# Loads, vector order and token slots around the last product of a cross-attention output projection

## The chip, the core and the metric

The kernel runs on one core of a Trainium2 chip. The metric is the device time of one execution in microseconds (us), over several runs of the same program. One further execution was taken with the hardware profiler, and every row below comes from it. The engines are called by the profile's names: PE (TensorE), DVE (VectorE), ACT (ScalarE), POOL (GpSimd) and SP (SyncE, which here only issues DMAs).

## What is computed

One encoder layer over 512 tokens of width 1024 in float32. The part that matters here is its last third: memory cross-attention, its output projection `w_xo`, a norm, and a SwiGLU feed-forward network.

```python
def memory_cross_attention(hn, memn, w_q, w_k, w_v, w_o):
    ...
    s = jnp.einsum('blhd,bmhd->bhlm', q, k).astype(jnp.float32) * (XATTN_HEAD_DIM ** -0.5)
    p = jax.nn.softmax(s, axis=-1).astype(v.dtype)
    o = jnp.einsum('bhlm,bmhd->blhd', p, v).reshape(bsz, seq, D_MODEL)
    return o @ w_o

def swiglu(hn, w_gate, w_up, w_down):
    return (jax.nn.silu(hn @ w_gate) * (hn @ w_up)) @ w_down
...
        h = h + memory_cross_attention(rms_norm(h, xattn_norm_g[i]), memn, ...)
        h = h + swiglu(rms_norm(h, ffn_norm_g[i]), w_gate[i], w_up[i], w_down[i])
    return rms_norm(h, final_norm_g)
```

## The kernel before

Every matrix product is made of three matmuls (`mm3`): each operand is split into a high half (`hi`, a cast on ACT, line 85) and a low half (`lo`, a subtraction on DVE, line 86), and hi x hi, hi x lo and lo x hi are summed in PSUM. So each block of weights (512 KB) takes a DMA, a cast of about 1 us and a subtraction of about 1.2 us before PE can use it.

**The plan.** All weight blocks stand in one list, `plan`, in the order in which they are used. `next_w` takes the next block. On its way it starts the loads of later blocks (`begin`: a block of the plan is loaded `LOADS` = 3 positions ahead, those of a feed-forward unit at distances of their own) and splits blocks up to `SPLITS` = 2 positions ahead. `FAR` is how far down the list it looks for loads that are due. Raw blocks share three buffers (tag `raw`), and so do the high and the low halves (tags `hi`, `lo`). The framework's scheduler then orders the instructions of each engine, DMA issues on SP included, by a simulated timeline; `in_order` pins an instruction behind the one written before it on its engine, and `pinned[0]` turns that on for `split` and `sum_sq`.

**The products.** `w_xo` and the feed-forward units are multiplied by a Strassen-like scheme of seven products, P1 to P7, over sums of quarter blocks. `w_xo` takes each product in two halves c, which makes fourteen plan positions, counted here from 0: P1 c0, P7 c0, P1 c1, P7 c1, P6 c0 (4), P5 c0 (5), P6 c1 (6), P5 c1 (7), P4 c0, c1 (8, 9), P2 c0, c1 (10, 11), P3 c0, c1 (12, 13). Behind them stand a block of `w_gate` (14), P1 of feed-forward unit 0 (15), a second block of `w_gate` (16), P2 of unit 0 (17), two blocks of `w_up` (18, 19), and P5 of unit 0 (20). A half product of `w_xo` is 12 matmuls of 512 columns.

The weights of a unit come from four loads: `b11` (P1), `b21` (P2), and `t` and `b22` (P5). `t` is loaded by SP, and a second block is then added onto it by a DMA that POOL issues (line 181). `b21`, `t` and `b22` live in the pool `units`, which is opened where the attention pool `ap_` has been closed and takes its memory. The operands of P5 and P6 of `w_xo` lie in two tiles of `ap_` (`kt_hi`, `kt_lo`), and so `ap_` is closed after P5.

**The norm between.** When both halves of a row of `h` are complete, `half_done` squares them (ACT, line 499). `to_fn` makes the factor (DVE `ms`, POOL `r`), scales the row into `xs` (DVE, line 525), and somewhat later `to_feat` transposes `xs` on PE (`ptr`, line 533, 8 for a token tile) and splits it into `fn_hi` and `fn_lo` (ACT, DVE) and a copy `full` (ACT, line 537). Tokens 0 and 1 (256 rows, T0) come before tokens 2 and 3 (T1). The feed-forward stage begins with half products on T0 alone (`gate_part(0, T0)`, `unit_start`, `gate_part(1, T0)`, `unit_second`, 24 matmuls of 256 columns each), and goes on to T1 after that. `between()` is one matmul whose result is not used.

`fn` and `hn`, like `xn` at the start, are the two views of one tile with the tag "B" (`token_slot`).

**The softmax.** `scores` divides each row of probabilities by its sum on DVE (line 1270), four instructions of 128x256 for a head.

Of the kernel before, what the change touches and what calls it, by code (L numbers as in the profile page):

```python
# [10 lines left out]
F32R = mybir.dt.float32r  # L11
AF = mybir.ActivationFunctionType
# [5 lines left out]
P = 128  # L18
# [34 lines left out]
def hybrid_layer_kernel(  # L53
# [41 lines left out]

    LOADS, SPLITS, FAR = 3, 2, 7
    plan, tiles = [], []

    def block(w, kb, k, c0, n):
# [15 lines left out]
    def halves_at(t, k, n, off):  # L117

        return tuple(t[:, i * k * n + o:(i + 1) * k * n + o].rearrange("p (k n) -> p k n", k=k)
                     for i, o in enumerate(off))  # L120
# [38 lines left out]

    stp = [None]  # L160

    def plan_unit(w, c0, ordered=False):

        kh = KD // 2
        b = lambda i, j: block(w, i * kh, kh, c0 + 256 * j, 256)
        r = {}

        def fresh(nm):
            r[nm] = (wp if nm == "b11" else stp[0]).tile([P, kh, 256], F32, tag="raw" if nm == "b11" else nm,
                                                         name=nm, bufs=3 if nm == "b11" else 2)  # L170
            return r[nm]

        def plain(nm, src):
            def f():
                ins = nc.sync.dma_start(fresh(nm), src)
                if ordered:
                    in_order(ins)
            return f

        def onto(nm, src):  # L180
            return lambda: nc.gpsimd.dma_start(r[nm], src, accum_op=ALU.add)

        def tt(o, x, y, op):
            nc.vector.tensor_tensor(r[o], r[x], r[y], op)

        def make(nm, *then):
            def f():
                ops = halves(r[nm])
                if then:
                    tt(*then)  # L190
                return ops
            return f

        return {q: ((w, c0, q), loads, made) for q, loads, made in (
            (1, [(4, plain("b11", b(0, 0)))], make("b11")),
            (2, [(4, plain("b21", b(1, 0)))], make("b21")),
            (5, [(7, plain("t", b(0, 0))), (5, onto("t", b(0, 1))), (5, plain("b22", b(1, 1)))],
             make("t", "t", "t", "b22", ALU.add)),
            (6, [], lambda: (make("t", "b11", "t", "b11", ALU.subtract)(), tt("t", "t", "b21", ALU.add))[0]),
            (7, [], make("b11")),  # L200
            (4, [], make("t")),
            (3, [], make("b22")))}
# [42 lines left out]
    def plan_units(units, down):  # L245


        made = [plan_unit(*u, ordered=i == 1) for i, u in enumerate(units)]
        for i in range(2):
            plan_block(w_gate, 4 * i, 4, FS, 256, place=i + 1)  # L250
            plan.append(made[0][i + 1])
        plan_feat(w_up, FS, KD)
        for i, m in enumerate(made):
            nx = made[i + 1] if i + 1 < len(made) else {}
            between = [nx[1]] if nx else down[:1]
            plan.extend([m[5], m[6]] + between + [m[7], nx[2] if nx else down[1], m[4], m[3]])
        plan.extend(down[2:])
# [288 lines left out]
    def slot(tag, shape, dt, name):  # L546
        return sp.tile(list(shape), dt, tag=tag, name=name)

    def token_slot(name, off=(0, 0)):

        return halves_at(sp.tile([P, 2 * KD * T + 128], F32R, tag="B", name=name), KD, T, off)


    s5 = ExitStack()
# [589 lines left out]
    h = slot("A", (P, NT, D), F32, "h")  # L1144
    for t in range(NT):
        nc.sync.dma_start(h[:, t, :], x[t * P:(t + 1) * P, :])
    hn_hi, hn_lo = token_slot("hn", APART)

    def mq_tile(name, off):
        return ap_.tile([P, KD * M + 64], F32R, tag="mq", name=name, bufs=2)[:, off:off + KD * M]  # L1150
# [98 lines left out]
    def scores(hd):  # L1249
        q_hi, q_lo = qs.pop(hd)  # L1250
        scale = XD ** -0.5
        prob = ap_.tile([P, NT, M], F32, tag="prob", name="prob", bufs=1) if hd % 2 == 0 else \
            np_.tile([P, NT, M], F32, tag="gain", name="prob", bufs=2)
        for i in range(2):
            ps = bank("psc").rearrange("p (t m) -> p t m", t=2)
            for tt in range(2):
                t = 2 * i + tt
                tsl = slice(t * P, (t + 1) * P)
                for k in range(2):
                    mm3(ps[:, tt, :], (q_hi[:, k, tsl], q_lo[:, k, tsl]),  # L1260
                        (kt_hi[:, 2 * hd + k, :], kt_lo[:, 2 * hd + k, :]), k == 0, k == 1)
            mx, nm, sm, rs = (ap_.tile([P, 2], F32, tag=k, name=k, bufs=4) for k in ("mx", "nm", "sm", "rs"))
            nc.vector.tensor_reduce(mx, ps, AX.X, ALU.max)
            nc.vector.tensor_scalar(nm, mx, -scale, None, ALU.mult)
            for tt in range(2):
                nc.scalar.activation(prob[:, 2 * i + tt, :], ps[:, tt, :], AF.Exp, bias=nm[:, tt:tt + 1],
                                     scale=scale, accum_out=sm[:, tt:tt + 1])
            nc.vector.reciprocal(rs, sm)
            for tt in range(2):
                nc.vector.tensor_scalar(prob[:, 2 * i + tt, :], prob[:, 2 * i + tt, :], rs[:, tt:tt + 1], None, ALU.mult)  # L1270
        return prob

    def turn_probs(hd, prob):
# [138 lines left out]
    def onto(ps, t0, half, op):  # L1412
        for t in range(2):
            hs = h[:, t0 + t, HALF[half]]
            nc.vector.tensor_tensor(hs, hs, ps[t], op)

    def half_done(t, half):
        sum_sq(hss[:, 1, t, half:half + 1], h[:, t, HALF[half]])
# [1 line left out]
    values(0, *pts.pop(0))  # L1420
    probs2 = scores(2)
    probs3 = scores(3)
    for q, nm in ((5, "kt_hi"), (6, "kt_lo")):
        s_ = ap_.tile([P, KD, M], F32R, name=nm).rearrange("p (i k) t -> p i k t", i=2)
        xops[q] = s_[:, 0], s_[:, 1]
    turn(1, probs1)
    ox = [bank("ox0"), bank("ox1")]
    xo_product(ox, 1, 0, True, False)
# [8 lines left out]
    values(3, *pts.pop(3))  # L1437
    xo_product(oy, 7, 1, False, True)
    onto(oy, 0, 1, ALU.subtract)
    oq = [bank("oq0"), bank("oq1")]  # L1440
    xo_product(ox, 6, 0, False, False)
    xo_product(oq, 5, 0, True, False)
    xo_product(ox, 6, 1, False, True)
    onto(ox, 0, 1, ALU.subtract)
    xo_product(oq, 5, 1, False, True)
    at.close()
    ff = ExitStack()
    fp = ff.enter_context(tc.tile_pool(name="ffn", bufs=1))
# [1 line left out]
    sx = ExitStack()  # L1450
    stp[0] = sx.enter_context(tc.tile_pool(name="units", bufs=2))
    full = fp.tile([P, KD, T], F32, tag="full", name="full", bufs=1)
    onto(oq, 0, 1, ALU.add)
    onto(ox, 0, 0, ALU.add)
    for t in range(2):
        half_done(t, 1)
    onto(ox, 2, 1, ALU.subtract)
    xo_product(oy, 4, 0, False, False)
    xo_product(oy, 4, 1, False, True)
    fn_hi, fn_lo = token_slot("fn", APART)  # L1460
    fn = (fn_hi, fn_lo)
    to_fn = feat_norm(g_f, fn_hi, fn_lo, full)
    for t in range(2):
        hs = h[:, t, HALF[0]]
        nc.vector.tensor_tensor(hs, hs, oy[t], ALU.add)
        half_done(t, 0)
        to_fn(t, hss[:, 1, t, :])
    ov = [bank("ov0"), bank("ov1")]
    xo_product(ov, 2, 0, True, False)
    xo_product(ov, 2, 1, False, True)  # L1470
    onto(ov, 2, 0, ALU.add)
    for t in (2, 3):
        half_done(t, 0)

    ws = [next_w(w_xo, 3, c) for c in range(2)]
    for t in range(2):
        for c in range(2):
            xo_product(oq, 3, c, False, c == 1, ws[c], (t,))
        hs = h[:, 2 + t, HALF[1]]
        nc.vector.tensor_tensor(hs, hs, oq[t], ALU.add)  # L1480
        half_done(2 + t, 1)
        to_fn(2 + t, hss[:, 1, 2 + t, :])

# [134 lines left out]
    for i, u in enumerate(UNITS):  # L1620
        final = i == len(UNITS) - 1
        x, v = begun
        q = unit_bank("pq")
        product(q, u, 5, True, ops)
        if final:
            last_job.append(u)
            make_tokens(1, 0)
        if i == 0:
            split(*fn_q(K0, T1), s3)
            between()  # L1630
        product(x, u, 6, False, ops)
        u2 = stp[0].tile([P, 2, 256], F32, tag="u2", name="u2", bufs=2)
        u3 = np_.tile([P, 2, 256], F32, tag="ev", name="u3", bufs=2)
        nc.scalar.copy(u2, x)
        if not final:
            begun = unit_start(UNITS[i + 1])
        else:
            dx = [bank(f"dx{t}") for t in range(2)]
            down_product(dx, 1, True, range(1))
        product(x, u, 7, False, ops)  # L1640
        nc.scalar.copy(u3, x)
        if i == 0:
            sum4()
        if not final:
            unit_second(UNITS[i + 1], begun[1])
        else:
            down_product(dx, 1, True, range(1, 2))
        V.tensor_tensor(u3, q, u3, ALU.subtract)
        put(u, 1, T1, u3)
        product(x, u, 4, False, ops)  # L1650
        put(u, 0, T1, x)
        if u[0] is w_up:
            a_, b_ = (acts(u[1] // 512, f)[:, :, T1] for f in (0, 1))
            V.tensor_tensor(a_, a_, b_, ALU.subtract)
        product(q, u, 3, False, ops)
        V.tensor_tensor(u2, q, u2, ALU.subtract)
        put(u, 1, T0, u2)
# [131 lines left out]
```

## Time and profile before

| | |
|---|---|
| median of 3 runs | 908.13 us (906.52 to 908.89) |
| profiled execution | 908.21 us, of which the span is 906.4 us |
| PE busy | 889.8 us, 98% of the span |
| DVE busy | 643.9 us, 71% |
| ACT busy | 488.1 us, 54% |
| POOL busy | 111.0 us, 12% |
| DMA moved | 165.35 MB, mean 182 GB/s |

Shares are over the whole span. The changed code stands between 505 and 610 us of it: heads 2 and 3 of the softmax at about 515 to 525 us, `w_xo` from 520 to 572 us, and the first feed-forward blocks behind it. A matmul of 512 columns shows 389 to 394 ns from its start to its end, but the next one starts 0.23 us after it, since they are pipelined; rows that join several instructions give the time from the first start to the last end.

### The profile page before, as it was taken

To read this page: it belongs to the slowest core of one execution; us is meant where nothing else is said; L and a number is where in the kernel's file an instruction comes from. 1 tells how busy PE (TensorE), PEld (TensorE's weight loads), DVE (VectorE), ACT (ScalarE), POOL (GpSimd) and SP (SyncE) were. 2 spreads that over 40 slices of the span, in tenths; PEclk is the share of its full clock that TensorE was granted. 3 is DMA by queue.
4 is the path that set the end of the run, shared out by engine and by line. 5 is a ranking of instruction groups with operands and counts; after the bars stand their busy time and mean duration, and the time that the engine had idled before them with its cause. 6 is when DMAs were issued, how large, how long until landed. Compare 5 with 4: busy or idle time off the path is not lost.

```text
span 906.4 us, 14551 instructions
## 1 busy us (share of the span) xinstructions
PE 889.8 (98%) x5620; PEld 785.7 (87%) x5620; DVE 643.9 (71%) x1048; ACT 488.1 (54%) x716; POOL 111.0 (12%) x173
## 2 busy tenths in 40 slices
PE   9999999999999999999999999899999999999996
PEld 6788888888888887889989987799999999988885
DVE  5596662888853125867956898886778777898875
ACT  5542985244375233446655675655554554665664
POOL 1003420110025300011000001101121111000010
PEclk9999999999999999999999999999999999999999
DMA  7556574587546568883569627628698999367672
GB/s 240 164 141 191 119 181 143 156 216 162 140 125 150 135 182 245 247 275 96 163 208 267 175 70 234 208 52 228 166 275 221 212 229 244 96 181 232 201 232 95
DMA packets 116167, 165.35 MB, mean 182 GB/s; under 512 B 13873, under 2 KB 78913, under 8 KB 116034
## 3 DMA queue, kind: packets, MB, share of 16 engines
q1 hardware_dynamic: 95234, 134.56, 45.7%
q0 software_dynamic: 18272, 28.81, 19.4%
q10 hardware_dynamic: 2592, 1.05, 0.5%
q8 instruction: 44, 0.72, 0.3%
q14 instruction: 25, 0.20, 0.1%
HBM read 157.61 MB, written 46.63 MB: 225 GB/s over the span
## 4 chain that ended last, share of the span: by engine, by line
PE 84%; DMA 4%; ACT 4%; DVE 4%; issue 2%; POOL 0%; SPq 0%; ACTq 0%; POOLq 0%; DVEq 0%
PE pf L374 27%; PE px L1301 12%; PE pt L374 11%; PE dx L374 6%; PE pq L1301 6%; PE pv L1301 3%; PE qx L1301 2%; PE dq L374 2%; PE pk L813 2%; PE po L374 1%; PE psc L374 1%; PE qq L1301 1%; PE ptr L533 1%; DVE wlo L86 1%; PE dv L374 1%
## 5 line engine op out<-in xcount | busy, mean ns | idle before, releaser
L86 DVE TENSOR_TENSOR wlo<-wraw,whi 128x1024 fp32r<-128x1024 f32 (+1 forms) x147 | 174.7, 1189 | 106.3 <-ACT whi L85 104.4
L85 ACT CAST whi<-wraw 128x1024 fp32r<-128x1024 f32 (+1 forms) x147 | 150.6, 1025 | 171.7 <-PE pf L374 67.4
L374 PE MATMUL pf<-xn,whi 128*128 128x512 f32 x448 | 140.1, 392 | 0.0
L374 PEld LDWEIGHTS pf<-xn,whi 128*128 128x128 f32 x448 | 83.4, 188 | 17.0 <-issue 0.2
L374 PE MATMUL pf<-xn,wlo 128*128 128x512 f32 x224 | 87.4, 390 | 0.0
L1301 PE MATMUL px<-fn,whi 128*128 128x256 f32 x480 | 83.2, 276 | 0.0
L1301 PEld LDWEIGHTS px<-fn,whi 128*128 128x128 f32 x480 | 72.5, 188 | 0.2
L85 ACT CAST whi<-b 128x1024 fp32r<-128x1024 f32 x40 | 42.1, 1054 | 49.2 <-PE px L1301 26.0
L86 DVE TENSOR_TENSOR wlo<-b,whi 128x1024 fp32r<-128x1024 f32 x40 | 48.8, 1223 | 26.2 <-ACT whi L85 26.2
L1301 PE MATMUL px<-fn,wlo 128*128 128x256 f32 x240 | 66.3, 276 | 0.0
L1301 PE MATMUL pq<-s,whi 128*128 128x256 f32 x320 | 55.0, 276 | 0.0
L374 PE MATMUL dx<-whi,s 128*128 128x512 f32 x170 | 53.7, 391 | 0.4 <-DVE h L1714 0.4
L374 PEld LDWEIGHTS pf<-xn,wlo 128*128 128x128 f32 x224 | 42.1, 188 | 8.8
L85 ACT CAST whi<-t 128x1024 fp32r<-128x1024 f32 x30 | 31.6, 1054 | 31.8 <-PE pv L1301 10.9
L86 DVE TENSOR_TENSOR wlo<-t,whi 128x1024 fp32r<-128x1024 f32 x30 | 36.7, 1225 | 16.5 <-ACT whi L85 16.5
L1301 PEld LDWEIGHTS pq<-s,whi 128*128 128x128 f32 x320 | 48.2, 188 | 0.0
L1301 PEld LDWEIGHTS px<-fn,wlo 128*128 128x128 f32 x240 | 45.1, 188 | 0.0
L374 PE MATMUL pt<-whi,xn 128*128 128x512 f32 x128 | 44.4, 419 | 0.1
L1301 PE MATMUL pq<-s,wlo 128*128 128x256 f32 x160 | 44.2, 276 | 0.0
L374 PEld LDWEIGHTS dx<-whi,s 128*128 128x128 f32 x170 | 31.8, 188 | 7.4 <-issue 0.8
L374 PE MATMUL dx<-wlo,s 128*128 128x512 f32 x85 | 33.1, 391 | 0.5 <-DVE wlo L86 0.5
L294 POOL DMA_DIRECT2D dsum<-in_w_down_dram x12 | 13.9, 1158 | 133.9 <-DMA dsum<-in_w_down_dram 130.1
(459 smaller groups left out, 2265.4 us busy)
## 6 DMA issues: line engine op xcount, KB each, us to landing
wraw<-in_w_in_dram SPq DMA_DIRECT2D x36, 512.0 KB, 4.3
dsum<-in_w_down_dram SPq DMA_DIRECT2D x20, 512.0 KB, 5.5
wraw<-dsum SPq DMA_DIRECT2D x20, 512.0 KB, 4.2
b<-in_w_gate_dram SPq DMA_DIRECT2D x15, 512.0 KB, 5.0
b<-in_w_up_dram SPq DMA_DIRECT2D x15, 512.0 KB, 4.9
wraw<-in_w_down_dram SPq DMA_DIRECT2D x15, 512.0 KB, 4.7
dsum<-in_w_down_dram POOLq DMA_DIRECT2D x10, 512.0 KB, 7.7
dsum<-dsum POOLq DMA_DIRECT2D x10, 512.0 KB, 7.2
```

Of the source, the lines that this page charges most:

```text
L85: hi = nc.scalar.copy(dst_hi, src)
L86: lo = nc.vector.tensor_tensor(dst_lo, src, dst_hi.bitcast(F32), ALU.subtract)
L294: plan[j + step][1].append((0, lambda d=dst, x=more: nc.gpsimd.dma_start(d, x, accum_op=ALU.add)))
L374: m = nc.tensor.matmul(ps, a[x], b[y], start=start and i == 0, stop=stop and i == 2, skip_group_check=free)
L533: nc.tensor.transpose(ps[:, j, :], src[:, k * P:(k + 1) * P], ident)
L813: nc.tensor.matmul(ps[32 * j:32 * j + 32, q, :], bd[i][:, g].rearrange("p d c -> p (d c)"), lc(es[i], g), start=(i == 0), stop=False, tile ...
L1301: nc.tensor.matmul(ps[:, j, :], a[x], b[y], start=start and j == k == i == 0, stop=k == 3 and i == 2, skip_group_check=True)
```

## The change

1. `FAR` goes from 7 to 15, and `plan_unit` takes `ahead`, which is 8 for unit 0 and 0 for the others. `b21` and `t` of unit 0 are then due at position 5 and not 13, the accumulation onto `t` and `b22` at position 7 and not 15. `b11` keeps its distance.
2. The operands of P5 and P6 of `w_xo` go into a slot "C". `ap_` is closed, and `units` and the feed-forward pool are opened, before P6 c0 and not after P5 c1.
3. `token_slot` takes two tiles, "B" and "C", of half the size each.
4. From behind P6 c1 to behind P2 c1, `pinned[0]` is set, and the additions onto `h` (`onto`) then keep their written order too. Some additions and squares are written in another order. `to_fn` of tokens 0 and 1 stands between P2 c0 and P2 c1.
5. P3 is multiplied half by half for both token tiles, not token tile by token tile, with the additions and `to_fn` of tokens 2 and 3 behind it.
6. The second `between()` (of unit 0's P6) is gone.
7. Heads 2 and 3 are scaled by an ACT instruction (Copy with a scale), not on DVE.

```diff
-    LOADS, SPLITS, FAR = 3, 2, 7
+    LOADS, SPLITS, FAR = 3, 2, 15
...
-            (2, [(4, plain("b21", b(1, 0)))], make("b21")),
-            (5, [(7, plain("t", b(0, 0))), (5, onto("t", b(0, 1))), (5, plain("b22", b(1, 1)))],
+            (2, [(4 + ahead, plain("b21", b(1, 0)))], make("b21")),
+            (5, [(7 + ahead, plain("t", b(0, 0))), (5 + ahead, onto("t", b(0, 1))), (5 + ahead, plain("b22", b(1, 1)))],
...
-        made = [plan_unit(*u, ordered=i == 1) for i, u in enumerate(units)]
+        made = [plan_unit(*u, ordered=i == 1, ahead=8 * (i == 0)) for i, u in enumerate(units)]
...
-    def token_slot(name, off=(0, 0)):
+    def token_slot(name, off=0):
-        return halves_at(sp.tile([P, 2 * KD * T + 128], F32R, tag="B", name=name), KD, T, off)
+        return tuple(sp.tile([P, KD * T + 64], F32R, tag=tag, name=name)[:, off:off + KD * T].rearrange(
+            "p (k t) -> p k t", k=KD) for tag in ("B", "C"))
...
-                nc.vector.tensor_scalar(prob[:, 2 * i + tt, :], prob[:, 2 * i + tt, :], rs[:, tt:tt + 1], None, ALU.mult)
+                row = prob[:, 2 * i + tt, :]
+                if hd < 2:
+                    nc.vector.tensor_scalar(row, row, rs[:, tt:tt + 1], None, ALU.mult)
+                else:
+                    nc.scalar.activation(row, row, AF.Copy, scale=rs[:, tt:tt + 1])
...
-            nc.vector.tensor_tensor(hs, hs, ps[t], op)
+            add = nc.vector.tensor_tensor(hs, hs, ps[t], op)
+            if pinned[0]:
+                in_order(add)
...
-    for q, nm in ((5, "kt_hi"), (6, "kt_lo")):
-        s_ = ap_.tile([P, KD, M], F32R, name=nm).rearrange("p (i k) t -> p i k t", i=2)
-        xops[q] = s_[:, 0], s_[:, 1]
+    os_ = slot("C", (P, 4, 4, 256), F32R, "os")
+    xops[5], xops[6] = (os_[:, 0], os_[:, 1]), (os_[:, 2], os_[:, 3])
...
+    oq = [bank("oq0"), bank("oq1")]
+    xo_product(ox, 6, 0, False, False)
+    xo_product(oq, 5, 0, True, False)
+    xo_product(ox, 6, 1, False, True)
+    pinned[0] = True
+    onto(ox, 0, 1, ALU.subtract)
+    xo_product(oq, 5, 1, False, True)
     onto(oq, 0, 1, ALU.add)
-    onto(ox, 0, 0, ALU.add)
     for t in range(2):
         half_done(t, 1)
+    onto(ox, 0, 0, ALU.add)
+    xo_product(oy, 4, 0, False, False)
     onto(ox, 2, 1, ALU.subtract)
-    xo_product(oy, 4, 0, False, False)
     xo_product(oy, 4, 1, False, True)
+    onto(oy, 0, 0, ALU.add)
+    for t in range(2):
+        half_done(t, 0)
+    ov = [bank("ov0"), bank("ov1")]
+    xo_product(ov, 2, 0, True, False)
...
     for t in range(2):
-        hs = h[:, t, HALF[0]]
-        nc.vector.tensor_tensor(hs, hs, oy[t], ALU.add)
-        half_done(t, 0)
         to_fn(t, hss[:, 1, t, :])
-    ov = [bank("ov0"), bank("ov1")]
-    xo_product(ov, 2, 0, True, False)
     xo_product(ov, 2, 1, False, True)
+    pinned[0] = False
...
     ws = [next_w(w_xo, 3, c) for c in range(2)]
-    for t in range(2):
-        for c in range(2):
-            xo_product(oq, 3, c, False, c == 1, ws[c], (t,))
-        hs = h[:, 2 + t, HALF[1]]
-        nc.vector.tensor_tensor(hs, hs, oq[t], ALU.add)
-        half_done(2 + t, 1)
-        to_fn(2 + t, hss[:, 1, 2 + t, :])
+    for c in range(2):
+        xo_product(oq, 3, c, False, c == 1, ws[c])
+    onto(oq, 2, 1, ALU.add)
+    for t in (2, 3):
+        half_done(t, 1)
+        to_fn(t, hss[:, 1, t, :])
...
             split(*fn_q(K0, T1), s3)
-            between()
         product(x, u, 6, False, ops)
```

More of the change, by code (lines that the diff above doesn't have):

```diff
@@ L160, in hybrid_layer_kernel, with plan_unit @@
     stp = [None]
-    def plan_unit(w, c0, ordered=False):
+    def plan_unit(w, c0, ordered=False, ahead=0):
         kh = KD // 2
@@ L1146, in hybrid_layer_kernel @@
         nc.sync.dma_start(h[:, t, :], x[t * P:(t + 1) * P, :])
-    hn_hi, hn_lo = token_slot("hn", APART)
+    hn_hi, hn_lo = token_slot("hn", APART[0])
     def mq_tile(name, off):
@@ L1439, in hybrid_layer_kernel @@
     onto(oy, 0, 1, ALU.subtract)
[L1440 to L1445, printed above, removed]
     at.close()
@@ L1452, in hybrid_layer_kernel @@
     full = fp.tile([P, KD, T], F32, tag="full", name="full", bufs=1)
+    oq = [bank("oq0"), bank("oq1")]
[5 more added lines that the diff above has]
+    xo_product(oq, 5, 1, False, True)
     onto(oq, 0, 1, ALU.add)
-    onto(ox, 0, 0, ALU.add)
     for t in range(2):
         half_done(t, 1)
+    onto(ox, 0, 0, ALU.add)
+    xo_product(oy, 4, 0, False, False)
     onto(ox, 2, 1, ALU.subtract)
-    xo_product(oy, 4, 0, False, False)
     xo_product(oy, 4, 1, False, True)
-    fn_hi, fn_lo = token_slot("fn", APART)
+    onto(oy, 0, 0, ALU.add)
[3 more added lines that the diff above has]
+    xo_product(ov, 2, 0, True, False)
+    fn_hi, fn_lo = token_slot("fn", APART[0])
     fn = (fn_hi, fn_lo)
```

## Prediction

> **What bounds the kernel now.** PE is busy for 98% of the span, so only time in which PE does not multiply can be won. I looked first for such time near the change: the waits of PE, window 505 to 612 us (engine, line, releaser; total, times, longest).
>
> ```profile
> PE ptr L533 <- ACT full L537: 1.6, 1, 1.6
> PE oq L374 <- DVE wlo L86: 1.5, 2, 1.1
> PE pf L374 <- ACT fn L85: 0.6, 1, 0.6
> ```
>
> Together 3.7 us. The windows by stretch (second number PE busy, then PEld, DVE, ACT, POOL; near the end PEclk, the granted clock) show a second loss:
>
> ```profile
> 569.00:572.00 3.00, 2.04 (x9) 1.70 (x10) 3.00 (x3) 2.52 (x4) 0.00 (x0) 1.00 0.27 66
> 572.00:575.00 3.00, 1.11 (x6) 0.51 (x4) 3.00 (x5) 2.26 (x4) 0.00 (x0) 1.00 0.85 265
> 575.00:578.00 3.00, 2.75 (x14) 2.67 (x15) 2.89 (x5) 1.74 (x4) 0.00 (x0) 0.63 0.07 24
> 578.00:581.00 3.00, 3.00 (x23) 3.00 (x22) 1.88 (x6) 2.68 (x7) 0.40 (x1) 0.80 0.61 193
> ```
>
> After the gaps the clock fell to 0.63. The chain of waits, 555 to 593 us (start, us, what), shows its price and where the gaps come from:
>
> ```profile
> 554.47 1.23 DVE wlo L86
> ...
> 555.72 6.29 DMA wraw<-in_w_xo_dram
> ...
> 562.11 1.06 ACT whi L85
> ...
> 563.19 1.23 DVE wlo L86
> ...
> 569.93 3.72 DMA wraw<-in_w_gate_dram
> ...
> 573.67 1.04 ACT s L85
> ...
> 575.91 4.24 PE pf L374 x22
> 580.15 2.71 PE px L1301 x23
> ```
>
> 22 matmuls took 4.24 us, where the next 23 took 2.71 (0.118 each): 4.24 - 22 x 0.118 = 1.65 us lost to the clock. The load of P3 c0 is issued at 555.72, behind the subtraction of position 9 that frees its raw buffer, and needs 6.29 us. Why so late and so long: DVE's timeline, SP's timeline, SP's waits.
>
> ```profile
> 550.89 3.66 DVE L1415 TENSOR_TENSOR h<-h,ox 128x512 f32<-128x512 f32 x6
> 554.47 1.22 DVE L86 TENSOR_TENSOR wlo<-wraw,whi 128x1024 fp32r<-128x1024 f32 x1
> ```
> ```profile
> 553.32 0.37 SPq L175 DMA_DIRECT2D b<-in_w_gate_dram  x1
> 553.74 0.50 SPq L175 DMA_DIRECT2D t<-in_w_gate_dram  x1
> 554.29 0.50 SPq L175 DMA_DIRECT2D b<-in_w_gate_dram  x1
> 555.72 2.10 SPq L241 DMA_DIRECT2D wraw<-in_w_xo_dram  x2
> ```
> ```profile
> SPq L175 <- PE oq L374: 2.5, 1, 2.5
> ```
>
> Six additions stood ahead of position 9's subtraction, whose cast was done at 552.1. Three loads of unit 0, which had waited for P5 to leave the attention pool, were issued just ahead of w_xo's last two, and the DMA engines were at 0.94 to 1.10 of their time from 554 to 568 us. ACT, in order, waited 3.33 us for that load (its timeline), and the squares of tokens 0 and 1 behind it came at 563.07, though their additions ended at 560.4. All three waits of PE follow: the late `lo` of P3 c0, that of P3 c1 behind `xs`, and the late `fn` of tokens 0 and 1, whose last transposes wait for an aux bank that ACT frees only after a cast waiting for a `w_gate` load.
>
> **The change, part by part.**
>
> *Loads eight positions sooner, operands in slot C.* The same four transfers of 512 KB move from 553-561 us to about 541-556 us: the last attention matmul (`po`) ends at 540.8, and P5 and P6 no longer hold that memory. In 540-547 the DMA engines are busy 0.24, in 547-554 0.66, so there is room. On SP they pass position 9's load (546.31) and positions 10 and 11 (549.25 on); on POOL the accumulation passes only `r`, about 15 us later. Their cost is 0 if SP is not held (rival D if it is). The gain is that P3 c0's load meets free engines, say 4.5 us (median landing of these loads) for 6.29.
>
> *Pinned order.* Additions take 0.60 us, subtractions 1.14, from start to start. DVE from 550.9: two additions 552.1, lo of position 9 553.3 (for 555.7 before), two 554.5, two 555.7, lo 10 556.8, two 558.0, lo 11 559.2, the two onto P4 (its last matmul ends at 558.9) 560.4. Position 12 is then loaded from 553.3 and lands near 557.8, for 562.0. ACT: the squares end at 561.1, the pinned cast of 12 at 562.1; lo 12 ends at 563.3. PE wants it at 564.0 (in the run before it began P3 c0 at 563.53 and its second kind of matmul would have come 0.46 later). What stands behind the pinned waits is lo 12 and lo 13, and PE waits for those; spare 0.7 us. Then r (two of 0.55 on POOL) is done by 562.5, `xs` takes 4 x 0.67 to 566.0, lo 13 to 567.1, against 566.7 plus the transposes put in between. So the 1.5 us go.
>
> *fn of tokens 0 and 1.* With P3 (24 x 0.23 = 5.5 us) and 16 transposes (4 groups of 0.44) PE is through at about 571.0. DVE has from 563.3 to 571.0, 7.7 us, for `xs` 2.7, lo 13 1.1, four `fn` lo 2.4, two additions of P2 1.2 and the lo of position 14, 1.1: 8.5 us. It is late by about 0.9. The gap is then too short for the clock to fall, by the run before: 12 transposes and 1.14 us of waiting (567.3 to 570.0) left it at 1.00. So 1.6 + 0.6 + 1.65 us go, but for 0.9.
>
> The Trainium skill, page "TensorE: Matmul & The Clock Gate" (Part 1 on the clock gate, Part 4 on transposes), says that a free-running window of about 3.4 us with too little PE work halves the clock, and that transposes do not count as such work. The trace agrees as far as it goes: 572.5 to 575.9 us held three matmuls and four transposes, and 0.63 followed. By that rule the transposes in a row and 0.9 us of waiting might be enough; that is rival B.
>
> *P3 half by half.* PE ran it so before too, c0 for both tiles first, since lo 13 was missing: 0. *One idle matmul fewer:* 0.23. *Two tiles for the slot:* same bytes, same views; nothing in `xn`'s or `hn`'s stages waits for the slot: 0.
>
> *Scaling of heads 2 and 3 on ACT.* DVE loses 8 x 0.28 (L1270: four in 1.12) = 2.2 us, in a stretch where it idles (0.32, 0.23, 0.86 us). ACT gains 8 of 128x256; not in the trace in this form, bounded by a cast of 128x256 (0.37) and an Exp of that shape (0.47): 3.0 to 3.8 us. ACT's idle pieces there are 1.60 + 1.40 + 1.24, and head 2's last `p_lo` (ended 528.3) is wanted at 530.5: 0, taken nearest to that spare of 2.2 us. If nothing is covered, 1.6 us on PE; a gain is excluded, since PE has no wait there.
>
> *Sum:* 1.5 + 1.6 + 0.6 + 1.65 + 0.23 = 5.6; less 0.9, 4.7. Behind it PE multiplies without a wait from 593 to 797 us, so nothing later takes it back. 908.2 - 4.7 = 903.5 us (profiled execution; the median lies 0.1 lower). A measurement here tells 0.3%, 2.7 us, from no change.
>
> **What is late next** is `fn` of tokens 2 and 3. PE needs it after four half products (11.3 us) and 16 transposes (1.8), from 571.9 on: 585.0. DVE from 571.0 has additions 1.2, `xs` 2.7, `fn` 2.4, five weight lo 5.7: 583.0 if it never waits. Spare 2.0 us.
>
> **Rivals.**
> B, *the clock falls again*: the T0 wait stays near 0.9 us and the bunched transposes bring 0.63 back: 903.5 + 1.65 = 905.1. For: 3.4 us nearly without matmuls did it before. Against: 2.7 us did not.
> C, *tokens 2 and 3 become the bound*: before, their `fn` ended 18.6 us after P3's last matmul (572.1 to 590.7), with DVE idle for 4.4 us of it. With that idle, 587.4: PE waits 2.4 us, 905.9. With the full 18.6, 571.0 + 18.6 = 589.6: 4.6 us, 908.1. Middle 907. Against: part of the idle was ACT waiting for late loads.
> D, *SP is held* (slower): `b21` and `t` now stand ahead of w_xo's own loads. If their memory comes free only with P5 (552.9), as in the row above, position 9's load goes from 546.3 to 552.9, lands at 557.4, and its lo comes at 559.6, where PE wants it at 556.0: 3.6 us. Positions 10 and 11 then meet the four transfers, 6.3 for 4.5 us, 1.8 each: 7.2, and with the clock's 1.65 it is 8.9 against 5.6 won: 911.5. It decides from a release later than about 549 us. For: exactly this wait is in the trace. Against: the operands that caused it have moved to slot C.
> E, *no effect*, the scheduler ordering SP as before: 908.2.
>
> **Chances.** Forecast 0.52, B 0.15, C 0.13, D 0.17, E 0.03. B lies at the edge of 0.3%: two thirds of it faster. Faster 0.52 + 0.10 = 0.62, same 0.05 + 0.13 + 0.03 = 0.21, slower 0.17. Range: from 902.0 (5.6 won without the 0.9, and 0.6 more: after each wait the next matmul came 0.1 us later than in a run without one, 0.34 after 564.47, and the sum leaves that out) to 910.9, the edge of slower, which takes in C, E and the uncovered ACT work on top of B, and leaves out most of D.
>
> **What would show it.** Right: PE's waits in 540-580 us total under 1.2 us; PEclk 1.00 in every stretch; P3 c0's load issued near 553.3 and landed by 558; `b21` and `t` issued near 541; P5 of unit 0 starting near 602 (606.83 before). Wrong: `b`/`t` rows on SP waiting for PE (D), a wait of `pf` on `fn` near 585 (C), a clock below 1 near 572 (B), PE waiting for `p_hi` or `p_lo` near 530 (ACT).

## The result: 911.1 us against 907.6 us, slower

Over 20 runs each, after took a median of 911.12 us (909.53 to 917.74) and before 907.60 us (904.90 to 909.50). The ratio of the mean times is 1.0052, interval 1.0037 to 1.0068. The forecast was 903.5 us, and "faster". The profiled spans are 910.1 us (after) and 906.4 us (before), at the same mean granted clock of 0.995.

Where the time went is read from PE's timeline, by five points that both kernels pass. All are counted from the first `pf` matmul of the program (44.66 us before, 43.11 us after: the code up to there is the same, and that 1.6 us is chance, as the runs below show it at 42.4 to 45.0).

| point on PE | before | after | after - before |
|---|---|---|---|
| last matmul of P4 | 513.65 | 513.24 | -0.4 |
| last matmul of P2 | 518.64 | 520.76 | +2.1 |
| second group of `px` on T0 | 535.33 | 532.47 | -2.9 |
| P5 of unit 0 | 562.01 | 565.59 | +3.6 |
| last `px` | 750.13 | 753.52 | +3.4 |

So 2.5 us are lost at P2 (some 0.45 us of that only because before had put two matmuls of P2 ahead of the last ones of P4), 5.0 us are won between P2 and the first products on T0, close to the forecast for that stretch, and 6.5 us are lost between those and P5 of unit 0. Nothing happens after that up to the last `px`. (Behind it, ACT waited 5.65 us for one load at 822 us, where it waited 1.91 us in before, and the rest of the program took 109.6 us against 107.7 us. In the other traces of these experiments it took 107.6 to 108.9 us.)

The waits of PE in after, window 505 to 620 us (engine, line, releaser; total, times, longest):

```profile
PE pf L375 <- ACT fn L85: 3.3, 1, 3.3
PE ov L375 <- DVE h L1421: 1.8, 1, 1.8
PE idle L1567 <- ACT fn L85: 0.7, 1, 0.7
PE oq L375 <- DVE wlo L86: 0.5, 1, 0.5
PE ptr L534 <- ACT full L538: 0.3, 1, 0.3
```

The three waits of before at P3 and at `fn` of tokens 0 and 1 have shrunk from 3.7 to 0.8 us. Two new ones stand above them: P2 waits for an addition onto `h`, and the first `pf` on tokens 2 and 3 waits for a cast of `fn`. The windows by stretch in after (PE, PEld, DVE, ACT, POOL; then PEclk):

```profile
572.00:576.00 4.00, 3.65 (x32) 3.45 (x31) 4.00 (x5) 2.91 (x6) 0.00 (x0) 1.00 0.41 123
...
584.00:588.00 4.00, 1.12 (x11) 0.89 (x9) 3.20 (x4) 3.97 (x6) 1.32 (x1) 0.90 1.09 348
588.00:592.00 4.00, 2.94 (x11) 2.45 (x12) 2.88 (x4) 2.97 (x6) 0.00 (x0) 0.50 0.94 141
592.00:596.00 4.00, 4.00 (x28) 4.00 (x28) 1.23 (x1) 0.70 (x1) 0.00 (x0) 0.74 0.00 0
```

Over the first products on T0 the clock is 1.00, where it fell to 0.63 in before. But from 584 to 588 us PE is busy for 1.12 us of 4, with ACT busy for 3.97, and the clock then falls to 0.50. The chain of waits in after over that stretch, then ACT's timeline in after, and then in before:

```profile
578.35 2.72 PE pf L375 x24
...
583.45 0.45 PE ptr L534 x4
583.92 0.24 ACT fn L85
...
584.41 0.33 ACT whi L85
...
585.36 0.59 ACT fn L85
585.96 1.28 ACT L1546
587.26 0.60 ACT a_up L1546
587.86 0.49 ACT fn L85
588.38 0.80 PE pf L375 x2
```
```profile
576.74 1.06 ACT L85 CAST whi<-wraw 128x1024 fp32r<-128x1024 f32 x1 [1.83 <-DMA wraw<-in_w_up_dram]
577.70 0.62 ACT L500 ACTIVATE sq<-h 128x512 f32<-128x512 f32 x1
...
583.92 0.59 ACT L85 CAST fn<-ptr 128x512 fp32r<-128x512 f32 x1 [2.75 <-PE ptr L534]
584.41 1.05 ACT L85 CAST whi<-t 128x1024 fp32r<-128x1024 f32 x1
585.36 0.59 ACT L85 CAST fn<-ptr 128x512 fp32r<-128x512 f32 x1
585.96 1.28 ACT L1546 ACT_TABLE_LOAD   x1
587.26 0.60 ACT L1546 ACTIVATE a_up<-pv 128x512 f32<-128x512 f32 x1
587.75 0.58 ACT L85 CAST fn<-ptr 128x512 fp32r<-128x512 f32 x1
```
```profile
584.30 1.55 ACT L85 CAST fn<-ptr 128x512 fp32r<-128x512 f32 x3
...
589.38 0.59 ACT L85 CAST fn<-ptr 128x512 fp32r<-128x512 f32 x1 [1.83 <-PE ptr L533]
590.23 1.05 ACT L85 CAST whi<-t 128x1024 fp32r<-128x1024 f32 x1 [0.27 <-PE pv L1301]
591.31 1.28 ACT L1538 ACT_TABLE_LOAD   x1
```

Between the casts of `fn` that PE waits for, ACT has three things that PE does not need yet: the cast of `t` (wanted at P5 of unit 0, 24 us later), the table load for Silu, and a Silu. Together they take 1.05 + 1.28 + 0.60 = 2.9 us, of the wait of 3.3 us. In before, ACT had the other order: all four casts of `fn` stood ahead of the cast of `t` and the table load. In after, the squares of the first of these tokens also stand late, at 577.70, behind a cast that waits 1.83 us for a load of `w_up`.

The loads and the queues: SP's timeline, SP's waits, and DVE's timeline in after.

```profile
538.30 0.38 SPq L176 DMA_DIRECT2D b<-in_w_gate_dram  x1
538.74 0.50 SPq L176 DMA_DIRECT2D t<-in_w_gate_dram  x1
...
539.84 0.43 SPq L176 DMA_DIRECT2D b<-in_w_gate_dram  x1
```
```profile
SPq L176 <- PE po L375: 7.4, 1, 7.4
```
```profile
550.88 0.69 DVE L1421 TENSOR_TENSOR h<-h,ox 128x512 f32<-128x512 f32 x1 [1.37 <-PE ox L375]
...
557.70 1.28 DVE L1421 TENSOR_TENSOR h<-h,ox 128x512 f32<-128x512 f32 x2
```

The three loads are issued at 538.3 to 539.8 us (553.3 to 554.3 before), as soon as the last `po` is through. SP stands still for 7.4 us until then, and PE has no wait for a block of weights between 505 and 558 us. The pinned additions are spread over 551 to 559 us as planned. The last pair of P6, at 557.70, frees the two PSUM banks into which P2 writes, and PE was through with P4 at 556.6.

### The profile page after: what moved, and what is told of

The parts are those of the page before. It is cut to its first block, busy times and chain, and to the rows that moved or that the text cites. A ratio compares the mean times of both kernels' runs of the same rounds, so it can differ in the third digit from the quotient of the medians.

```text
span 910.1 us, 14545 instructions
## 1 busy us (share of the span) xinstructions
PE 890.3 (98%) x5619; PEld 784.7 (86%) x5619; DVE 641.6 (70%) x1040; ACT 491.0 (54%) x724; POOL 111.9 (12%) x173
## 3 DMA queue, kind: packets, MB, share of 16 engines
q10 hardware_dynamic: 2592, 1.05, 0.4%
## 4 chain that ended last, share of the span: by engine, by line
PE 85%; ACT 5%; DVE 4%; DMA 3%; issue 2%; POOL 1%; ACTq 0%; POOLq 0%; SPq 0%; DVEq 0%
PE pf L375 27%; PE px L1307 12%; PE pt L375 11%; PE pq L1307 6%; PE dx L375 5%; PE pv L1307 3%; PE qx L1307 2%; PE dq L375 2%; PE pk L815 2%; DMA wraw<-dsum 1%; ACT whi L85 1%; DVE wlo L86 1%; PE ptr L534 1%; PE po L375 1%; PE ox L375 1%
```

## The experiments

Two kinds of question were open: which part of the change made the two new waits, and what each wait costs. The first four kernels ran on one chip, the next four on a second and the last four on a third. In every comparison the kernel before ran on the same chip; its median was 906.13 us (25 runs) for the first four kernels, 906.34 us (35) for the next four and 906.47 us (29) for the last four. A ratio is that of the mean times. "P5 at" is the start of P5 of unit 0, counted from the first `pf` as in the table above, in the profiled execution.

| kernel | median us (runs) | ratio to before, interval | P5 at |
|---|---|---|---|
| no pinned order | 910.68 (6) | 1.0051, 1.0034 to 1.0068 | 564.2 |
| loads not sooner | 910.99 (8) | 1.0085, 1.0049 to 1.0121 | 565.6 |
| scaling on DVE | 910.20 (12) | 1.0065, 1.0040 to 1.0091 | 564.8 |
| T1 pinned | 906.07 (12) | 1.0019, 0.9994 to 1.0044 | 559.6 |
| `up` cast pinned | 909.70 (12) | 1.0045, 1.0021 to 1.0068 | 559.4 |
| Silu's table early | 907.02 (12) | 1.0011, 1.0000 to 1.0022 | 562.1 |
| T1 pinned, additions first | 910.61 (12) | 1.0029, 1.0003 to 1.0055 | 559.4 |
| T1 pinned, scaling on DVE | 910.08 (12) | 1.0020, 0.9993 to 1.0047 | 558.0 |
| T1 pinned, idle matmuls | 905.77 (12) | 0.9994, 0.9979 to 1.0010 | 559.7 |
| the same, scaling on DVE | 904.56 (12) | 0.9979, 0.9966 to 0.9992 | 558.4 |
| after, with `between()` back | 911.57 (6) | 1.0054, 1.0035 to 1.0073 | 565.6 |
| before, without `between()` | 906.16 (12) | 0.9993, 0.9978 to 1.0008 | 559.8 |

Some of these medians hide two groups of times; that is the subject of experiments 7 to 10.

**1. After without the pinned order.**

```diff
-    pinned[0] = True
     onto(ox, 0, 1, ALU.subtract)
```

> The changed kernel with its pinning taken out: from P6 c1 to P2 c1 the splits, squares and additions are free to be reordered again; all else stays. Theory A (the T1 chain: in the changed kernel PE reaches the first products of tokens 2 and 3 sooner, and their fn is not there because ScalarE has other work in front of their squares and casts): the T1 wait of 3.3 us, the fall of the clock behind it and so most of the loss stay, 909.5 to 911.5 us. Theory B (the fixed order is the cause, by P2's wait of 1.8 us for its banks and what follows from it): 906 to 908 us, and no wait of ov.

Measured: 910.68 us. The waits of PE in this kernel, 505 to 620 us:

```profile
PE ptr L534 <- DVE xs L526: 2.1, 1, 2.1
PE ptr L534 <- ACT full L538: 1.7, 1, 1.7
PE pf L375 <- ACT fn L85: 1.4, 1, 1.4
```

The waits at tokens 0 and 1 are back, with 5.2 us in these three rows (the clock fell to 0.60 and 0.54 from 572 to 580 us), and the wait of P2 for `h` is gone; P2 waits 0.7 us for a cast of weights instead. The wait at tokens 2 and 3 is gone too. PE comes there later, and ACT has the order of before: three casts of `fn` at 585.33 us and the fourth at 590.44 us, all ahead of the cast of `t` (591.31) and the table load (592.38). So the pinned order is what wins the time at T0, and the wait of P2 for a bank belongs to it. The total is what it was: what is won at T0 is lost at T1.

**2. After with the loads of unit 0 at their old distance.**

```diff
-        made = [plan_unit(*u, ordered=i == 1, ahead=8 * (i == 0)) for i, u in enumerate(units)]
+        made = [plan_unit(*u, ordered=i == 1, ahead=0) for i, u in enumerate(units)]
```

> The changed kernel with unit 0's loads at their old distances (b21 4, t 7, the accumulation and b22 5 positions ahead). Theory A: these loads decide only the gain at tokens 0 and 1, so P3 c0's load lands later and PE waits about 1.5 us more before 570 us, while its wait for tokens 2 and 3 becomes shorter by as much: 910 to 913 us. Theory C (the early transfers and accumulation collide with w_xo's own loads and are the cause): 906 to 908.5 us.

Measured: 910.99 us, with three of the eight runs at 918.3 to 919.5. Theory A's range holds this, but not for its reason, since the edit changes nothing on SP (its timeline):

```profile
538.10 0.38 SPq L176 DMA_DIRECT2D b<-in_w_gate_dram  x1
538.53 0.50 SPq L176 DMA_DIRECT2D t<-in_w_gate_dram  x1
539.63 0.43 SPq L176 DMA_DIRECT2D b<-in_w_gate_dram  x1
```

The scheduler issues these loads when their memory comes free. What moved them was the earlier end of the attention pool (SP waits for `po` in after, and waited for `oq` in before); `ahead` moved nothing. This run gave something else by accident. A load of `w_up` landed sooner, so that ACT squared T1 earlier (ACT's timeline):

```profile
575.09 1.05 ACT L85 CAST whi<-wraw 128x1024 fp32r<-128x1024 f32 x1 [0.36 <-DMA wraw<-in_w_up_dram]
576.04 0.63 ACT L500 ACTIVATE sq<-h 128x512 f32<-128x512 f32 x1
```

The squares come 1.7 us sooner than in after, and the wait of `pf` for `fn` is the same 3.3 us; behind the squares ACT has the order of after. Late squares alone are therefore not the cause.

**3. After with the scaling of heads 2 and 3 on DVE again.**

```diff
-                if hd < 2:
+                if hd < 4:
```

> The changed kernel with the scaling of heads 2 and 3 back on VectorE. Theory A and my forecast say that it is worth nothing: within 0.8 us of the changed kernel, 910.3 to 912. Theory D (the 3 to 4 us more on ScalarE delay everything behind): 907 to 909 us, and fewer waits of PE between 515 and 545 us.

Measured: 910.20 us, just outside the ranges of both theories, with three of twelve runs at 915.6 to 920.5. PE's wait of 1.8 us at P2 is gone; the one of 3.3 us at T1 stays. DVE's timeline shows why P2 is in time:

```profile
548.59 1.28 DVE L1421 TENSOR_TENSOR h<-h,ox 128x512 f32<-128x512 f32 x2
```

The additions start 2.3 us sooner; in after the first one waits 1.37 us for P6 on PE. From the first `pf` to P2's last matmul it is 518.30 us here and 520.76 in after. So in this trace the eight scalings on ACT are not free. At P5 of unit 0, 0.7 us of the 2.5 are left, and the run times do not show them. How the 3 us of ACT turn into late additions was not followed instruction by instruction.

**4. After with ACT's and DVE's splits and squares pinned at T1 too.**

```diff
+    pinned[0] = True
     gate_part(0, T0)
...
     gate_part(1, T0)
+    pinned[0] = False
```

> The changed kernel with its pinning taken up again from gate_part(0, T0) up to unit_second: ScalarE then keeps the written order, squares and fn casts of tokens 2 and 3 ahead of the casts of the two w_up blocks, of the table load and of the Silu. Theory A: fn of tokens 2 and 3 is ready by about 585 us, PE's wait of 3.3 us and the half clock behind it (some 3 us) go: 904.5 to 907.5 us. Theories B, C and D: nothing is won behind 570 us, 910 to 912 us.

Measured: 906.07 us, seven runs at 903.57 to 906.14 and five at 911.01 to 913.23. The waits of PE:

```profile
PE ov L375 <- DVE h L1421: 1.8, 1, 1.8
...
PE px L1307 <- DVE wlo L86: 0.3, 1, 0.3
PE pf L375 <- DVE fn L86: 0.2, 1, 0.2
```

Pinning alone, with no work removed, takes the wait at T1 from 3.3 to 0.2 us (and that of the idle matmul from 0.7 to 0.3 us), keeps the clock at 1.00 from 568 to 596 us, and brings P5 of unit 0 from 565.6 to 559.6 us. Order on the engines, not the amount of work, made that wait. Seven of the twelve runs lie in theory A's range or just below it; the other five are taken up in experiment 7.

**5. Only one cast pinned.** Which of the things ahead on ACT matters?

```diff
+            pinned[0] = i == 1
             ws.append((4 * i,) + next_w(w_gate, 4 * i, 4, FS, 256))
+            pinned[0] = False
```

> The changed kernel with one thing pinned more: the splits written at gate_part(1, T0), which are those of the first w_up block, so that this cast, which waits for its DMA, can't stand ahead of the squares of tokens 2 and 3 on ScalarE. The rest of the order is left to the scheduler. Theory A1 (the squares, queued behind a cast that waits for a load, make the T1 chain late): the squares end by about 577 us in place of 578.8, PE's wait for fn at about 585 us falls from 3.3 to under 1 us, and the clock stays: 905 to 908 us. Theory A2 (the table load and the Silu ahead of the fn casts make it late): the wait stays over 1.5 us, 908.5 to 911 us.

Measured: 909.70 us in the median, but again in two groups, six runs at 905.79 to 907.88 and six at 911.52 to 915.16. ACT's timeline, from the profiled execution of the lower group:

```profile
573.17 0.66 ACT L500 ACTIVATE sq<-h 128x512 f32<-128x512 f32 x1
...
581.05 1.94 ACT L85 CAST fn<-ptr 128x512 fp32r<-128x512 f32 x3 [1.72 <-PE ptr L534]
...
583.84 1.07 ACT L85 CAST whi<-t 128x1024 fp32r<-128x1024 f32 x1
584.93 1.28 ACT L1546 ACT_TABLE_LOAD   x1
```

Three casts of `fn` now stand ahead of the cast of `t` and the table load, and the wait of `pf` has gone; the idle matmul waits 1.1 us for the fourth. The lower group lies in A1's range and the trace shows A1's signs. But the squares, the table load and the Silu have all changed places with the casts, so this run does not say which of them mattered.

**6. The table load moved away.** A Silu of one column, whose result nobody uses, is issued ahead of P2, so that the table is loaded there.

```diff
+    warm2 = np_.tile([P, 1], F32, tag="ms", name="warm2", bufs=2)
+    in_order(nc.scalar.activation(warm2, mhalf, AF.Silu))
     ov = [bank("ov0"), bank("ov1")]
```

> The changed kernel with one tiny Silu on ScalarE placed just ahead of P2, so that the table load of 1.28 us is done some 25 us sooner and is no longer in the T1 chain. Theory A2: PE's wait for fn falls from 3.3 us to under 1.5 and the half clock behind it may go: 905.5 to 908.5 us. Theory A1: the squares are still late, 909 to 911 us.

Measured: 907.02 us, in one group (906.04 to 909.24). The wait at T1 is gone. Other waits have grown in its place at T0: `pf` 1.5 us for DVE's `fn` and 0.6 us for ACT's, `oq` 0.9 and 0.4 us. This is A2's range, but not a proof of A2: PE reaches the second group of `px` 3.0 us later than in after, and ACT's order is that of before, with all four casts of `fn` ahead of the cast of `t`. What separates the fourteen traces is the order as a whole. The four with the order of after (after and experiments 2, 3 and 11) have the wait of 3.3 us, and the ten with three or four casts of `fn` ahead of the cast of `t` do not have it.

**7. The additions that free P2's banks first.** On top of experiment 4, the additions of P6 and P5 go ahead of P4, the squares behind it.

```diff
     onto(oq, 0, 1, ALU.add)
-    for t in range(2):
-        half_done(t, 1)
     onto(ox, 0, 0, ALU.add)
-    xo_product(oy, 4, 0, False, False)
     onto(ox, 2, 1, ALU.subtract)
+    xo_product(oy, 4, 0, False, False)
     xo_product(oy, 4, 1, False, True)
+    for t in range(2):
+        half_done(t, 1)
```

> The kernel pin_t1 with the additions of P6 and P5 all written ahead of P4 and the squares of the first halves behind P4, so that the casts of positions 9 to 11 don't stand behind squares and P2's banks come free sooner. If P2's wait of 1.8 us (ov on VectorE's additions) comes from the written order inside the pinned stretch, it goes and nothing takes its place: 1.5 to 2 us below pin_t1. If the gap only moves to a later late subtraction: within 0.7 us of pin_t1.

Measured: 910.61 us, five runs at 903.74 to 905.65 and seven from 909.71 on. PE still waits 0.6 + 0.3 us at P2 instead of 1.8, the 0.6 us for a subtraction. By the lower groups (medians 905.2 here, 905.0 in experiment 4) nothing is won, as the second expectation said. The better answer to that wait is experiment 10.

This profiled execution fell into the upper group (a span of 911.2 us), and so it shows what the two groups are. Its window from 660 to 700 us and then that of experiment 4, whose profiled execution lies in the lower group:

```profile
660.00:700.00 40.00, 40.00 (x342) 40.00 (x341) 29.81 (x30) 19.81 (x24) 7.64 (x8) 1.00 0.93 229
```
```profile
660.00:700.00 40.00, 40.00 (x355) 40.00 (x354) 31.22 (x32) 21.28 (x26) 7.18 (x7) 1.00 0.96 232
```

PE is busy all the time and the granted clock is 1.00 in both, yet one has 342 matmuls there and the other 355. In PE's timeline they start 117.8 and 113.3 ns apart. The slower pace begins behind this short wait (PE's timeline), and it lasts to 788 us, where the next matmuls of 512 columns come:

```profile
610.16 0.39 PE L1307 MATMUL px<-fn,wlo 128*128 128x256 f32 x1 [0.30 <-DVE wlo L86]
```

From P5 of unit 0 to the last `px` it is 195.0 us here and 188.6 us in experiment 4, where PE starts 1565 matmuls from 611 us to the last `px`: 1565 x 4.5 ns = 7.0 us, against the 6.4 us measured. The medians of the two groups lie about 7 us apart (905.2 and 912.5 here), and their mean granted clocks do not differ (0.993 to 0.998 and 0.996 to 0.998). That the other runs of the upper groups are slow for the same reason is an inference: this is the only one that was profiled.

**8. T1 pinned, and the scaling on DVE.** The edits of 3 and 4 together.

> The kernel pin_t1 with heads 2 and 3 scaled on VectorE. The kernel dve_scale had no wait at P2 in its trace; if that was the scaling (ScalarE's casts coming later behind it), this one is 1 to 2 us below pin_t1; if it was chance, within 0.7 us of it.

Measured: 910.08 us, five runs at 901.95 to 904.91 and seven from 910.02 on. The lower group is the fastest so far (median 904.4, 0.6 us below that of experiment 4, on another chip), which does not decide between the two expectations. The wait at P2 is down to 0.8 us, and P2 ends 1.6 us sooner by the points on PE, which speaks for the scaling.

**9 and 10. A matmul of 512 columns behind the short wait.** Can a matmul of 512 columns end the slower pace? The first expectation below takes that from the trace of before, and there it is a misreading: the slower pace began at 580 us, but it had ended at four transposes at 588.74 us, and the 18 matmuls ahead of the idle one at 592.14 us took 2.04 us, 113 ns each. Two other traces do show it. In experiments 1 and 6 the 18 matmuls ahead of the idle matmul (at 593.30 and 590.35 us) took 2.12 us, 118 ns each, and behind it they start 113 ns apart. So `between()`, which is such a matmul, is called behind the place of the short wait, in two units, on top of 4 (experiment 9) and of 8 (experiment 10).

```diff
             begun = unit_start(UNITS[i + 1])
+            if i < 2:
+                between()
```

> The kernel pin_t1 with an idle matmul of 512 columns (between) more behind P1 of unit 1 and of unit 2. Runs of pin_t1 fell into two groups, 903.6 to 906.1 and 911.0 to 913.2 us. Theory R (a short stall inside the 256-column products can leave PE at a slower pace, 117 to 118 ns from one matmul to the next in place of 113, as the trace of a run of the upper group shows from 610 us to the end of the units, and a 512-column matmul ends that, as in the trace of before at 592 us): the upper group is gone, all runs 903.5 to 907 us. Rival (the groups come from the chip or from another place): some 4 in 10 runs stay at 911 to 913 us.

> The kernel pin_t1_dve_scale with the same two idle matmuls. Theory R: no run over 908 us, median 904.5 (the lower group of pin_t1_dve_scale was 902.0 to 904.9, plus 0.4 for the two matmuls), 1 to 2 us below the kernel before. Rival: half of the runs at 910 to 913 us.

Measured: 905.77 and 904.56 us. Experiment 10 is faster than before: its interval of 0.9966 to 0.9992 excludes no change. Neither has an upper group, though three runs of experiment 9 lie above the 907 us of its expectation, at 907.6 to 908.9. The four kernels with the wait of `px` and without these matmuls had 5, 6, 7 and 7 of 12 runs in it; with the matmuls it is 0 of 24, while the wait itself is still there (the waits of PE in experiment 10):

```profile
PE ptr L534 <- DVE xs L526: 0.5, 1, 0.5
...
PE px L1307 <- DVE wlo L86: 0.3, 1, 0.3
```

Two things limit this. No kernel with that wait and without the two matmuls ran on the chip of these two runs, so the rival that this chip does not fall into the slower pace stands. And in both profiled executions the matmuls were already 113 ns apart between the short wait and the added matmul, so no trace shows one of the added matmuls ending the slower pace.

The pair also prices the scaling on ACT where nothing else differs: 905.77 - 904.56 = 1.2 us (1.5 us by the means, with an interval of some 1.3 us to either side; in the profiles up to P2's last matmul, 520.39 - 518.40 = 2.0 us).

**11 and 12. The idle matmul that the change removes.** It is put back into after, and taken out of before.

```diff
             split(*fn_q(K0, T1), s3)
+            between()
```

> The changed kernel with the second between() of the kernel before put back. If the idle matmul is worth no more than its 0.23 us: 910 to 911.5 us in most runs, some at 917 to 918 as in the changed kernel (3 of 20). Theory R: the same median, no run over 914 us, if the stall that leaves the slow pace lies before unit 0's P6.

> The kernel before with the second between() taken out, the one part of the change alone. The forecast's term says 0.23 us less. Theory R says the same, since the kernel before has no stall of PE in the units behind its first between(): 0 to 0.5 us below the kernel before, and no group of slower runs.

Measured: 911.57 us for after with it, with the waits of after; 906.16 us for before without it, against 906.47. So it is not the cause. Its price of 0.23 us is too small to tell from these runs, whose interval for experiment 12 is 0.9978 to 1.0008. That none of the six runs of experiment 11 is over 914 us says little beside 3 of 20 in after. Experiment 12 showed something else. Its waits at T0 are those of before (1.5, 1.4 and 0.4 us), but the clock did not fall. The window of 576 to 580 us in experiment 12, and then in before:

```profile
576.00:580.00 4.00, 4.00 (x38) 3.98 (x36) 3.03 (x9) 2.94 (x7) 1.06 (x2) 1.00 0.76 239
```
```profile
576.00:580.00 4.00, 4.00 (x23) 4.00 (x24) 3.42 (x5) 3.54 (x8) 0.00 (x0) 0.60 0.28 93
```

P5 of unit 0 comes at 559.8 us there, and at 562.0 us in the trace of before.

## Why the prediction was wrong, step by step

**"What is late next" failed.** The prediction gave `fn` of tokens 2 and 3 a spare of 2.0 us, from a sum of DVE's work alone, "583.0 if it never waits". The cast that PE waited for last was on ACT, whose queue held a weight cast, a table load and a Silu ahead of it. None of them was in the sum. DVE was later than its sum too: it waited 0.85 us for a cast of weights and 0.63 us for `r`, and at 583.9 us it had the 2.4 us of `fn` still to do. PE came to these tokens at 585.1 us, as forecast (585.0). With the order right (experiment 4) the spare is about zero, not 2.0 us: waits of 0.2 and 0.3 us on T1's path remain. In before, ACT had the four casts of `fn` ahead of those three instructions, and PE came to T1 later. Which part of the change turned ACT's order round was not tried by itself; experiment 1, without the pinned order between P6 and P2, has the order of before.

**Rival C was right in kind, and too cheap.** It priced a wait of 2.4 to 4.6 us; the waits were 3.3 + 0.7 = 4.0 us. But the clock fell behind them. The 24 matmuls from 591.30 on took 4.19 us, where 24 of them had taken 2.72 us at 578.35: 1.5 us in that one group. By the points on PE the whole stretch lost 6.5 us, so 2.5 us or so beyond the waits. The step that failed here is that the prediction applied the clock's price at T0 (1.65 us) but not to the wait that would replace it. And C got a chance of 0.13 on a spare that only one engine had been asked for.

**No step covered P2.** The additions were pinned behind the subtractions, and the prediction counted only who waits for the subtractions. The additions also free PSUM banks, and P2 takes two of them: 1.8 us on PE.

**The scaling on ACT was taken at 0 and is 1.2 us.** The prediction's own bound, "if nothing is covered, 1.6 us", holds it. The spare of 2.2 us that covered it was that of one `p_lo`. By the traces the time shows elsewhere, in the additions some 25 us later.

**The gain at T0 was right in size, and partly for the wrong reason.** 5.0 us were won between P2 and the first products on T0, against a sum of 4.7 (0.23 of it further on). The pinned order does win the waits (experiment 1). But 1.65 us of the sum were the fallen clock, and experiment 12 shows nearly the same waits at full clock: that term came in one execution and not in another, and against the trace of experiment 12 the same stretch is shorter by 3.4 us, not 5.0. That the 5.0 us came out close to the sum is in part luck. (The 0.118 us a matmul against which the term was priced is itself the slower pace of experiment 7; against 0.1133 us it is 1.75 us.) A part of the base was chance too. The execution of 908.2 us was slower than the medians of before in all later runs (906.1 to 907.6 us). With both new waits mended, the scaling back on DVE and two idle matmuls added, the change is worth 906.47 - 904.56 = 1.9 us, not 4.7.

**The loads were right in effect, wrong in cause.** P3 c0's load was issued at 553.64 us (forecast 553.3), the early loads at 538 to 540 us (forecast near 541). Rival D did not happen: SP did wait for the attention memory, 7.4 us, but that ended at 538.3 us, 11 us before the point from which D decides. `ahead`, to which the prediction gave a part of the move, does nothing (experiment 2). The low half of P3 c0 came later than the 563.3 us of the forecast, at 566.5, since `xs` and an addition stood ahead of it on DVE; the transposes in between cover most of that, and 0.5 us are left.

**Rival B did not happen.** The clock at 568 to 576 us was 1.00. The prediction set a rule beside it, from the Trainium skill, page "TensorE: Matmul & The Clock Gate" (Part 1): a free-running window of about 3.4 us with too little PE work halves the clock. The wait of 3.3 us at T1 gave 0.50 in all four traces that have it (after, experiments 2, 3 and 11), while the broken gaps of before gave 0.60 in one trace and 1.00 in another (experiment 12). That agrees with a window whose phase is not fixed; what the phase hangs on was not tried.

**Left open.** Three of after's 20 runs took 917.7 us, 6.6 us over its median, as did three of eight in experiment 2 and three of twelve in experiment 3 (915.6 to 920.5 us). That is near the distance of the two paces, but none of these runs was profiled, and these kernels have no wait of `px`. P3 by halves against token tiles, and the two tiles of the slot, were not tried by themselves.

## What to carry to other kernels

When a wait is taken away, sum up every engine on the path of the next one, in its queue order, and not only the engine with the most work: here a table load and two instructions that PE did not need yet, with the fallen clock behind the wait, are most of 6.5 us lost, where 5.0 us had been won. An instruction that is pinned holds what it frees as well as what it makes, PSUM banks above all. A loss seen in one profiled execution that hangs on the clock can be a chance event until a second trace has it, and a wait that is long enough to bring the clock down must be priced with it.

## What was not expected of the hardware

TensorE has two paces for the same stream of 256-column matmuls, at the same granted clock of 1.00: 113.3 and 117.8 ns from start to start. A wait of 0.3 us was enough to change from the first to the second, in one trace (experiment 7) and not in five others with that wait, and the slower one then lasted for some 180 us, worth 6.4 us. It needs no wait: four transposes between the matmuls began it in experiment 6 (at 586.85 us) and ended it in before (at 588.74 us). Matmuls of 512 columns can end it: one did at 593.30 us in experiment 1 and one at 590.35 us in experiment 6. They need not: in experiment 7 the first group of `dx` at 788 us brought the faster pace back (113 ns from 791.24 us on), and the second one, at 794 us, the slower (118 ns from 796.36 us on). With two more such matmuls, at 0.23 us each, the slower groups of times were gone (0 of 24 runs, where 25 of 48 had been in them), but on a chip where the kernels without them were not run. What decides between the two paces is open.
